# A hybrid decoder layer on one core: the hand order of its mixers, with pieces of projections between the instructions of each recurrent step and more of them behind substitutions and decode attention

## The chip, the core and the metric

The kernel runs on one core of a Trainium2 chip. The core has a matmul engine (TensorE, PE in the profile; its weight loads are shown as PEld), a vector engine (VectorE, DVE), an activation engine (ScalarE, ACT), GpSimd (POOL) and SyncE (SP), which issues the DMAs. Each engine works through its own queue in order; semaphores tie the queues to each other. The metric is the device time of one execution in microseconds (us), as the median of several runs.

## The reference

One decoder layer of width 1024, for a prompt of 1024 tokens and for 8 decode requests of 8 tokens each, which share the weights (1088 columns of tokens in all):

```python
x = x + 0.5 * rms_norm(swiglu_ffn(rms_norm(x, ffn1_norm_pre), ffn1_w_up, ffn1_w_down), ffn1_norm_post)
m, nk, nv, nc, ns = parallel_mixers(rms_norm(x, mix_norm_pre), w_in, ...)
x = x + rms_norm(m, mix_norm_post)
x = x + 0.5 * rms_norm(swiglu_ffn(rms_norm(x, ffn2_norm_pre), ffn2_w_up, ffn2_w_down), ffn2_norm_post)
```

`parallel_mixers` projects h with one matrix into the attention's q, k, v, a gated DeltaNet's q, k, v (qkv), its output gate z, two small columns, and the gates gA and gB. Branch A is sliding-window attention (8 heads, 2 key heads, window 128, sinks); the decode requests attend to a cache. Branch B, for each of 4 heads of 128 channels:

```python
xb = silu(short_conv(qkvb, width 4))
a = strict_lower(k_beta @ k.T * decay) + eye          # within a chunk of tokens
k_cum, v_u = solve(a, [k_beta * exp(gc), v * beta])
def step(s, xs):                                       # from chunk to chunk
    v_new = v_u_n - k_cum_n @ s
    o = q_dec_n @ s + qk_n @ v_new
    s = s * g_tot_n + k_dec_n.T @ v_new
ob = rms_norm(o, dn_out_norm) * silu(z)
m = (sigmoid(gA) * (oA @ w_branch_a) + sigmoid(gB) * (oB @ w_branch_b)) @ w_out
```

All is float32.

## The kernel before

Tokens lie along the free dimension, in three column chunks, `CH`: 0 to 384, 384 to 768, 768 to 1088 (the last 64 are the decode tokens). A projection onto 128 channels is a *unit*: its weights are loaded (two DMAs), split into a high part (a cast on ACT, L115) and a remainder (a subtraction on DVE, L116), and for each chunk `gemm` (L134) makes three matmuls for each of 8 blocks of the width: L142, L143 and L144 in the profile. So a unit is 3 × 8 × 3 = 72 matmuls, of 384 or 320 columns.

The first feed-forward layer comes first, then the projections of attention's q, k, v; then the mixers; then the branches, the output projection, and the second feed-forward layer. The change touches the mixers alone.

In the mixers, PE's order is written out by hand (`tc.manual_schedule(engines={PE})`, L1421); the other engines' order is left to a scheduler, which sees PE's. Between the instructions of the chains PE is given pieces of projections from a queue: a list of generators, each one unit. `gemm_p` (L839) yields after every block of three matmuls with a cost of 0.0013 us per column and 0.04: 0.54 for 384 columns, 0.456 for 320. `fill(us)` (L844) takes pieces off the head of the queue until that many us are used up, by these costs, or the queue is empty. `finish` (L852) issues what is left of units. The units are of three kinds: `conv_unit` (a head's q, k or v: projection into `pa`, then on ACT and DVE the norm factor, the short convolution L872, L874, and a SiLU, L901, L902), `z_unit` (the output gate's projection, L915, L916), and `gate_unit` (gA, gB: a tanh on ACT, L930; in the third chunk DVE applies the norm factor first, L672).

The chains, in their order:

- `attention_prompt` (L1007): 16 items in 18 rounds; in a round the scores (`att_s`, L950), softmax on ACT and DVE (`softmax`, L821 to L833), transposes (`att_t`, L979) and the products with v (`att_v`, L995), of three successive items, and then a fill.
- `attention_sample` (L1020): decode attention. Four items with scores (L1033, L1034), two additions on DVE (L1036, L1037), and a softmax; a fill; transposes of the probabilities (L1046, L1047); a fill; the products (L1055 and on).
- For each of two pairs of heads, 0 and 1, then 2 and 3: `Head.first` (L1108: transposes of k at L1129 with the squares' sums on ACT, L1131, and DVE, L1132; decay matrices; products; the matrix of the triangular system); `invert` (L1387: the 32 × 32 blocks of both heads inverted by 31 dependent steps on DVE, a trip through DRAM, and a fill); `Head.second` (L1225: the rest of the inverse from L1237 on, the product at L1283, eight recurrent steps, the decode tokens' step, and the norm of the output with L1363, L1374 and L1376 to L1380).

`first` and `second` are generators. `together` (L1383) takes one step of either head in turn, and each `yield` gives the us of a fill: the larger of the two heads' numbers is filled once, after both.

A recurrent step c of one head has, on PE: L1305 (the state into v_new), L1297 (the next step's u), L1314 (k with v_new), L1323 and L1324 (the output). DVE makes the scaled v_new (L1307) which L1314 needs, and the new state (L1317, L1321 in the first step) which the output of the next and L1323 of the same buffer wait for; ACT copies v_new (L1309, needed by L1324) and the output (L1325). The instructions of the two heads alternate: one head writes the PSUM buffers `ph`, the other `py`. `pa` (three buffers) holds the projections.

Of the kernel before, what the change touches and what calls it, by code (L numbers as in the profile page):

```python
# [35 lines left out]
def body(ctx: ExitStack, tc: tile.TileContext, d):  # L36
# [766 lines left out]
    for hlf in range(2):  # L803
        ps = py()
        for j in range(4):
            n = hlf * 4 + j
# [30 lines left out]
    queue = []  # L837
# [6 lines left out]
    def fill(us):  # L844
        while us > 0 and queue:
            t = next(queue[0], None)
            if t is None:
                queue.pop(0)
            else:
                us -= t  # L850

    def finish(units):  # L852
        for u in units:
            if u in queue:
                queue.remove(u)
                drain(u)
# [150 lines left out]
    def attention_prompt():  # L1007
        n = len(items)
        for it in range(n + 2):
            if it < n:  # L1010
                att_s(it)
            if it >= 2:
                att_v(it - 2)
            if 1 <= it <= n:
                att_t(it - 1)
            fill(4.8 if it else 7.0)
        for t in range(4):
            nc.sync.dma_start(oad[t, :, :NPR], YA[t][:, :NPR])

    def attention_sample():  # L1020
# [5 lines left out]
        for it in range(4):  # L1026
# [3 lines left out]
            for b4 in range(4):  # L1030
                b = bg2 * 4 + b4
# [8 lines left out]
            softmax(sb.unsqueeze(1), vec[:, V_SKS + g2 : V_SKS + g2 + 1], st())  # L1040
        fill(8.0)
        ptbs = [YA[0][:, it * 256 : it * 256 + 256] for it in range(4)]
# [8 lines left out]
        for it in range(4):  # L1051
# [6 lines left out]
            for b4 in range(4):  # L1058
                b = bg2 * 4 + b4
# [38 lines left out]
    class Head:  # L1098
# [9 lines left out]
        def first(self):  # L1108
# [15 lines left out]
            for c0 in (0, 4, 8):  # L1124
                n = 4 if c0 < 8 else 1
# [26 lines left out]
            nc.scalar.activation(eR, QK[:, cs8], AF.Exp)  # L1152
            yield 2.0

# [15 lines left out]
            for j, c0 in enumerate((0, 4)):  # L1170
                D = Ds[j]
                pq, pt = pb(), pb()
                for i in range(4):
                    w, cs, ix = chunk_of(c0 + i, h)
                    nc.tensor.matmul(pq[:, i * P : i * P + P], kT_[:, cs], q[:, cs], start=True, stop=True)
                for i in range(4):
                    nc.tensor.transpose(pt[:, i * P : i * P + P], D[:, i * P : i * P + P], ident)
                nc.vector.tensor_tensor(out=wide(QK, c0), in0=pq, in1=D, op=ALU.mult)
                nc.scalar.copy(D, pt)
                nc.gpsimd.tensor_tensor(out=wide(q, c0), in0=wide(q, c0), in1=Es[j], op=ALU.mult)  # L1180
                yield 0.0
            for j, c0 in enumerate((0, 4)):
# [31 lines left out]
            nc.gpsimd.memset(U[:NSM, NPR:], 0.0)  # L1214
            yield 0.0
            for c0 in (0, 4, 8):
                n = 4 if c0 < 8 else 1
# [4 lines left out]
                nc.scalar.copy(wide(v, c0) if c0 < 8 else v8, p[:w, : n * P])  # L1222
            yield 0.0

        def second(self):  # L1225
# [8 lines left out]
            for j in range(2):  # L1234
# [3 lines left out]
                nc.scalar.copy(Xs[j], p1)  # L1238
            yield 0.0
            for j in range(2):  # L1240
# [7 lines left out]
                nc.vector.tensor_tensor(out=wide(L, 4 * j), in0=wide(L, 4 * j), in1=p3, op=ALU.subtract)  # L1248
            yield 0.0
            p4s = [pb(), pb()]  # L1250
            for j in range(2):
# [6 lines left out]
                nc.scalar.copy(Xh, p4[:64, 0:256].rearrange("p (i c) -> p i c", c=64))  # L1258
            yield 0.0
            for j in range(2):  # L1260
# [17 lines left out]
            nc.scalar.mul(U[:w, cs], U[:w, cs], bhr[:w, 8:9])  # L1278
            yield 2.0
            for j in range(2):  # L1280
# [6 lines left out]
            nc.scalar.mul(mq[:, :NSM], p5[:, :w], -1.0)  # L1287
            yield 0.0

# [9 lines left out]
            uv(0)  # L1299
            yield 0.0  # L1300
            for c in range(8):
                w, cs, ix = chunk_of(c, h)
                p = ps[c]
                if c > 0:
                    nc.tensor.matmul(p[:, 0:128], M[:, cs], S, start=False, stop=True)  # L1305
                vns = ar[:, c % 2, :]
                nc.vector.tensor_scalar_mul(vns, p[:, 0:128], tk["kds"][:, ix : ix + 1])  # L1307
                vn = ar[:, 2 + c % 2, :]
                nc.scalar.copy(vn, p[:, 0:128])  # L1309
                yield 0.0  # L1310
                if c < 7:
                    uv(c + 1)
                yield 0.0
                nc.tensor.matmul(p[:, 128:256], k[:, cs], vns, start=True, stop=True)  # L1314
                S2 = ar[:, 4 + c % 2, :]
                if c > 0:
                    nc.vector.scalar_tensor_tensor(  # L1317
                        out=S2, in0=S, scalar=tk["gtot"][:, ix : ix + 1], in1=p[:, 128:256], op0=ALU.mult, op1=ALU.add
                    )
                else:  # L1320
                    nc.vector.tensor_copy(S2, p[:, 128:256])  # L1321
                if c > 0:
                    nc.tensor.matmul(p[:, 256:384], S, q[:, cs], start=True, stop=False)  # L1323
                nc.tensor.matmul(p[:, 256:384], vn, QK[:, cs], start=c == 0, stop=True)  # L1324
                nc.scalar.copy(QK[:, cs], p[:, 256:384])  # L1325
                S = S2
                yield 0.0
            nc.sync.dma_start(d["dpo"][h], S)
# [10 lines left out]
            nc.scalar.copy(ar[:, 0, :], p[:, 0:128])  # L1339
            yield 0.0  # L1340
            po = pb()
# [8 lines left out]
            for hf, vm in enumerate(vms):  # L1350
# [5 lines left out]
                )  # L1356
            yield 2.0
            nc.tensor.matmul(po[:, 128:192], vn, QK[:NSM, ss], start=True, stop=True)
# [11 lines left out]
            nc.sync.dma_start(d["dso"][:, h].rearrange("b p e -> p b e"), S0)  # L1370
            yield 5.0
            for a, b in ((0, 512), (512, 1024), (1024, NT)):
# [7 lines left out]
            nc.sync.dma_start(obd[h], QK)  # L1380
            yield 0.0

    def together(a, b):  # L1383
        for us in zip(a, b):
            fill(max(us))

    def invert(heads):  # L1387

        a, b = heads
# [17 lines left out]
        for i, x in enumerate(heads):  # L1407
# [6 lines left out]
            for b2 in range(2):  # L1414
                nc.sync.dma_start(U[32 * b2 : 32 * b2 + 32, NPR + 32 * b2 : NPR + 32 * b2 + 32], bu[h][32 + b2])
        fill(46.0)

# [3 lines left out]
    with tc.manual_schedule(engines={mybir.EngineType.PE}):  # L1421
        queue += zs[0:2] + gates[0:3] + heads[0].conv
        attention_prompt()
        attention_sample()
        queue += heads[1].conv
        for hs in (heads[0:2], heads[2:4]):
            finish(list(queue))
            queue += gates[3:9] if hs[0].h == 0 else gates[9:]
            together(*(x.first() for x in hs))
            invert(hs)  # L1430
            together(*(x.second() for x in hs))
            if hs[0].h == 0:
                finish(list(queue))
                queue += zs[2:4] + heads[2].conv + heads[3].conv
        finish(list(queue))
        wg4 = [unit(U_GA + i, f"ga{i}") for i in range(14, 16)]
        for c in range(3):
            for i in range(2):
                drain(gate_do(14 + i, wg4[i], c))
# [198 lines left out]
```

## Time and profile before

| | |
|---|---|
| median of 3 runs | 2466.16 us (2465.65 to 2466.87) |
| the profiled execution | 2460.59 us |
| its span, first to last instruction | 2458.8 us |
| mean granted clock of TensorE | 0.986 |
| prompt attention ends (last L995) | 973 us |
| decode attention, L1033 to the products | 1000 to 1020 us |
| first pair: first(), substitution, steps, tail | 1056.8 to 1206.2 us |
| between the pairs (gates, z, conv of heads 2 and 3) | 1206.2 to 1316.1 us |
| second pair | 1316.1 to 1463.2 us |

The profile's page gives each engine's busy time and the granted clock in 40 slices of 61 us; other views of the same trace group instructions by line, list what an engine waited for, give an engine's instructions in order of time, or sum each engine's busy time within stretches. Two peculiarities: matmuls are pipelined, so that the next one starts before the modelled end of the last, and durations of single matmuls overlap; starts are the safer measure. And a line of a helper (L142 to L144, L115, L116, L672) stands for all its callers; the tile's name (`h_ga`, `h_qkv`, `h_z`) tells them apart.

### The profile page before, as it was taken

How to read it: one execution, taken by the hardware profiler on the slowest of the kernel's cores; microseconds unless marked ns; L12 is line 12 of the kernel's file. 1: busy time of each engine (PE TensorE's matmuls, PEld its weight loads, DVE VectorE, ACT ScalarE, POOL GpSimd, SP SyncE). 2: the span in 40 equal slices, each digit the busy share in tenths (PEclk: the TensorE clock that was granted, in tenths of full speed). 3: DMA queues.
4: the chain of work that ended last, by engine and by line, in shares of the span. 5: the costliest groups of instructions: out<-in, count | busy, mean ns of one | idle time of the engine just before them, and what ended most of it. 6: DMA issues, size and time to landing. Idle time of an engine off the chain costs nothing. (4 is left out here: it accounts for less than half of the span.)

```text
span 2458.8 us, 38753 instructions
## 1 busy us (share of the span) xinstructions
PE 2372.7 (96%) x14535; PEld 2302.1 (94%) x14535; DVE 1691.8 (69%) x3385; ACT 1098.7 (45%) x2272; POOL 42.9 (2%) x33
## 2 busy tenths in 40 slices
PE   8999999999999999898999989999999999999997
PEld 7999999999998988898899879999989999999997
DVE  8887667767688467774477537655897476676677
ACT  7644424324466455443444343255654333233344
POOL 0000000000000000010101010000000000000000
PEclk9999999999999999899999999999999999999998
DMA  7332212213454411323322426435523122122453
GB/s 268 124 113 86 74 48 86 74 48 116 156 168 153 163 57 51 100 75 93 119 81 69 115 78 214 143 133 177 184 89 105 40 88 80 40 89 80 149 165 135
DMA packets 170373, 272.00 MB, mean 111 GB/s; under 512 B 34892, under 2 KB 74288, under 8 KB 170176
## 3 DMA queue, kind: packets, MB, share of 16 engines
q1 hardware_dynamic: 170184, 269.52, 34.1%
q8 instruction: 114, 1.87, 0.3%
q14 instruction: 75, 0.61, 0.1%
HBM read 227.03 MB, written 43.41 MB: 110 GB/s over the span
## 5 line engine op out<-in xcount | busy, mean ns | idle before, releaser
L467 PE MATMUL pa<-cl,h_c_s 128*128 128x384 f32 x704 | 236.3, 336 | 4.7 <-DVE cl L276 4.7
L466 PE MATMUL pa<-ch,h_c_s 128*128 128x384 f32 x704 | 237.3, 337 | 2.2 <-DVE t L472 1.8
L468 PE MATMUL pa<-ch,l_c_s 128*128 128x384 f32 x704 | 236.3, 336 | 0.0
L472 DVE TENSOR_TENSOR t<-pa,t 128x384 f32<-128x384 f32 x308 | 170.3, 554 | 85.1 <-PE pa L468 84.7
L466 PE MATMUL pa<-ch,h_c_a 128*128 128x384 f32 x528 | 177.2, 336 | 1.5 <-DVE t L472 0.8
L468 PE MATMUL pa<-ch,l_c_a 128*128 128x384 f32 x528 | 176.7, 335 | 0.0
L467 PE MATMUL pa<-cl,h_c_a 128*128 128x384 f32 x528 | 176.6, 334 | 0.0
L115 ACT CAST h_c_a<-r_c_a 128x512 fp32r<-128x512 f32 x132 | 81.8, 620 | 130.9 <-PE pa L467 107.7
L466 PEld LDWEIGHTS pa<-ch,h_c_s 128*128 128x128 f32 x704 | 132.9, 189 | 5.8 <-DVE t L472 5.5
L467 PEld LDWEIGHTS pa<-cl,h_c_s 128*128 128x128 f32 x704 | 133.0, 189 | 4.9 <-DVE cl L276 4.9
L468 PEld LDWEIGHTS pa<-ch,l_c_s 128*128 128x128 f32 x704 | 132.9, 189 | 0.0
L115 ACT CAST h_c_s<-q_c_s 128x512 fp32r<-128x512 f32 x132 | 82.0, 621 | 107.3 <-PE pa L467 96.8
L142 PE MATMUL pa<-xbh,h_ga 128*128 128x384 f32 (+1 forms) x384 | 128.3, 334 | 0.0
L144 PE MATMUL pa<-xbh,l_ga 128*128 128x384 f32 (+1 forms) x384 | 126.4, 329 | 0.0
L143 PE MATMUL pa<-xbl,h_ga 128*128 128x384 f32 (+1 forms) x384 | 126.3, 329 | 0.0
L466 PEld LDWEIGHTS pa<-ch,h_c_a 128*128 128x128 f32 x528 | 99.1, 188 | 2.8 <-DVE t L472 1.5
L467 PEld LDWEIGHTS pa<-cl,h_c_a 128*128 128x128 f32 x528 | 99.1, 188 | 0.0
L468 PEld LDWEIGHTS pa<-ch,l_c_a 128*128 128x128 f32 x528 | 99.1, 188 | 0.0
L142 PE MATMUL pa<-xbh,h_qkv 128*128 128x384 f32 (+1 forms) x288 | 95.9, 333 | 0.0
L143 PE MATMUL pa<-xbl,h_qkv 128*128 128x384 f32 (+1 forms) x288 | 95.0, 330 | 0.0
L144 PE MATMUL pa<-xbh,l_qkv 128*128 128x384 f32 (+1 forms) x288 | 94.9, 330 | 0.0
L115 ACT CAST h_c_s<-r_c_s 128x512 fp32r<-128x512 f32 x44 | 27.4, 622 | 147.9 <-PE pa L467 135.8
(630 smaller groups left out, 7271.0 us busy)
## 6 DMA issues: line engine op xcount, KB each, us to landing
r_c_a<-in_up_dram SPq DMA_DIRECT2D x132, 256.0 KB
q_c_a<-in_up_dram SPq DMA_DIRECT2D x44, 256.0 KB
q_ub<-in_up_dram SPq DMA_DIRECT2D x44, 256.0 KB
r_ub<-in_up_dram SPq DMA_DIRECT2D x44, 256.0 KB
r_ua<-in_up_dram SPq DMA_DIRECT2D x42, 256.0 KB
q_ua<-in_up_dram SPq DMA_DIRECT2D x42, 256.0 KB
r_da<-in_dn_dram SPq DMA_DIRECT2D x40, 256.0 KB
q_da<-in_dn_dram SPq DMA_DIRECT2D x40, 256.0 KB
```

The costliest lines, as they stand in the source:

```text
L115: nc.scalar.copy(hi, full)
L142: nc.tensor.matmul(ps[:, :n], hi[:, j, :], at(xh, k), start=first, stop=False)
L143: nc.tensor.matmul(ps[:, :n], hi[:, j, :], at(xl, k), start=False, stop=False)
L144: mm = nc.tensor.matmul(ps[:, :n], lo[:, j, :], at(xh, k), start=False, stop=last)
L466: nc.tensor.matmul(ps, wh[:, k, :], xh[:, k, :], start=k == 0, stop=False)
L467: nc.tensor.matmul(ps, wh[:, k, :], xl[:, k, :], start=False, stop=False)
L468: nc.tensor.matmul(ps, wl[:, k, :], xh[:, k, :], start=False, stop=k == 3)
L472: nc.vector.tensor_tensor(out=out, in0=ps, in1=other, op=ALU.add)
```

## The change

Five things are changed, all in the order of PE's instructions. No instruction is added or removed.

1. The fills of `attention_prompt` are 7.5 us in the first round and in the last two, 4.8 in the others.
2. One more gate unit is queued ahead of `attention_sample`, whose fill after the scores goes from 8 to 13 us; what is left in the queue then is issued before head 1's conv units are queued.
3. `together` fills after either head's step: a `yield` now carries two numbers, of which the first counts after head a and the second after head b. `first` has (2.0, 2.0) where it had one 2.0 for the pair; the steps of `second` get (0, 0.8) ahead of L1314 and (0, 0.5) at the end of a step, where nothing was filled; the fill before L1283 goes from 2.0 to 2.8.
4. The fill of `invert` goes from 46 to 51 us.
5. The queue of the first pair is gate units 4 to 9 (3 to 8 before), that of the second is the z units of heads 2 and 3 and gate units 10 to 13 (9 to 13 before); these z units no longer stand ahead of the conv units of heads 2 and 3.

```diff
-            fill(4.8 if it else 7.0)
+            fill(4.8 if 0 < it < n else 7.5)
...
-        fill(8.0)
+        fill(13.0)
...
             nc.scalar.activation(eR, QK[:, cs8], AF.Exp)
-            yield 2.0
+            yield 2.0, 2.0
...
             nc.scalar.mul(U[:w, cs], U[:w, cs], bhr[:w, 8:9])
-            yield 2.0
+            yield 0.0, 2.8
...
                 vn = ar[:, 2 + c % 2, :]
                 nc.scalar.copy(vn, p[:, 0:128])
-                yield 0.0
+                yield 0.0, 0.0
                 if c < 7:
                     uv(c + 1)
-                yield 0.0
+                yield 0.0, 0.8
                 nc.tensor.matmul(p[:, 128:256], k[:, cs], vns, start=True, stop=True)
...
                 S = S2
-                yield 0.0
+                yield 0.0, 0.5
             nc.sync.dma_start(d["dpo"][h], S)
...
-            yield 2.0
+            yield 0.0, 2.0
             nc.tensor.matmul(po[:, 128:192], vn, QK[:NSM, ss], start=True, stop=True)
...
-            yield 5.0
+            yield 0.0, 5.0
             for a, b in ((0, 512), (512, 1024), (1024, NT)):
...
     def together(a, b):
-        for us in zip(a, b):
-            fill(max(us))
+
+        for us in a:
+            fill(us[0])
+            fill(next(b)[1])
...
-        fill(46.0)
+        fill(51.0)
...
         attention_prompt()
+        queue += gates[3:4]
         attention_sample()
+        finish(list(queue))
         queue += heads[1].conv
         for hs in (heads[0:2], heads[2:4]):
             finish(list(queue))
-            queue += gates[3:9] if hs[0].h == 0 else gates[9:]
+            queue += gates[4:10] if hs[0].h == 0 else zs[2:4] + gates[10:14]
             together(*(x.first() for x in hs))
             invert(hs)
             together(*(x.second() for x in hs))
             if hs[0].h == 0:
                 finish(list(queue))
-                queue += zs[2:4] + heads[2].conv + heads[3].conv
+                queue += heads[2].conv + heads[3].conv
```

Every other `yield 0.0` of the two generators becomes `yield 0.0, 0.0`.

How the rows move is shown at three places. The first is a recurrent step of the first pair (c = 1) on PE. The names: `ph` is the PSUM buffer of head 0 and `py` that of head 1; `s_` are buffers in SBUF; `xbh`, `xbl` are the two parts of the normed input, `h_ga`, `l_ga` those of a gate unit's weights. Before:

```order
L1305 MATMUL ph_12195<-s_8355,s_8351 128x128
L1305 MATMUL py_12197<-s_8347,s_8345 128x128
L1297 MATMUL ph_12213<-s_8350,s_8353 128x128
L1297 MATMUL py_12215<-s_8344,s_8341 128x128
L1314 MATMUL ph_12195<-s_8355,s_8352 128x128
L1323 MATMUL ph_12195<-s_8348,s_8355 128x128
L1324 MATMUL ph_12195<-s_8354,s_8355 128x128
L1314 MATMUL py_12197<-s_8347,s_8340 128x128
L1323 MATMUL py_12197<-s_8342,s_8347 128x128
L1324 MATMUL py_12197<-s_8346,s_8347 128x128
```

The same step in the changed kernel, from L1297 to the second head's L1314:

```order
L1297 MATMUL ph_12375<-s_8350,s_8353 128x128
L1297 MATMUL py_12377<-s_8344,s_8341 128x128
L142 MATMUL pa_12298<-xbh_1_8284,h_ga_1_12096 128x320
L143 MATMUL pa_12298<-xbl_1_8286,h_ga_1_12096 128x320
L144 MATMUL pa_12298<-xbh_1_8284,l_ga_1_12097 128x320
L142 MATMUL pa_12298<-xbh_1_8284,h_ga_1_12096 128x320
L143 MATMUL pa_12298<-xbl_1_8286,h_ga_1_12096 128x320
L144 MATMUL pa_12298<-xbh_1_8284,l_ga_1_12097 128x320
L1314 MATMUL ph_12345<-s_8355,s_8352 128x128
L1323 MATMUL ph_12345<-s_8348,s_8355 128x128
L1324 MATMUL ph_12345<-s_8354,s_8355 128x128
L1314 MATMUL py_12347<-s_8347,s_8340 128x128
```

Six projection matmuls have come between L1297 and L1314 (three to six more follow the second head's L1324); between L1314 and L1323 there is none, before or now.

The second place is the tail of the first pair on PE, behind the decode tokens' products of L1366; `eye_72` holds the ones of L1374. Before, the 30 matmuls of a gate unit stood there, of which these are the last, and further ones behind L1374:

```order
L142 MATMUL pa_12453<-xbh_0_8283,h_ga_0_12135 128x320
L143 MATMUL pa_12453<-xbl_0_8285,h_ga_0_12135 128x320
L144 MATMUL pa_12453<-xbh_0_8283,l_ga_0_12136 128x320
L1374 MATMUL ph_12457<-s_8348,eye_72 128x512
L1374 MATMUL py_12460<-s_8348,eye_72 128x512
L1374 MATMUL ph_12463<-s_8348,eye_72 128x64
L1374 MATMUL py_12473<-s_8342,eye_72 128x512
L1374 MATMUL ph_12476<-s_8342,eye_72 128x512
L1374 MATMUL py_12479<-s_8342,eye_72 128x64
L142 MATMUL pa_12453<-xbh_0_8283,h_ga_0_12135 128x320
L143 MATMUL pa_12453<-xbl_0_8285,h_ga_0_12135 128x320
```

Now:

```order
L1366 MATMUL ph_12669<-s_8340,k_11427 128x512
L1366 MATMUL py_12672<-s_8340,k_11427 128x512
L1374 MATMUL ph_12676<-s_8348,eye_72 128x512
L1374 MATMUL py_12679<-s_8348,eye_72 128x512
L1374 MATMUL ph_12682<-s_8348,eye_72 128x64
L1374 MATMUL py_12692<-s_8342,eye_72 128x512
L1374 MATMUL ph_12695<-s_8342,eye_72 128x512
L1374 MATMUL py_12698<-s_8342,eye_72 128x64
L142 MATMUL pa_12720<-xbh_0_7321,h_qkv_0_12710 128x384
L143 MATMUL pa_12720<-xbl_0_7323,h_qkv_0_12710 128x384
L144 MATMUL pa_12720<-xbh_0_7321,l_qkv_0_12711 128x384
```

The queue is empty there, so L1374 follows L1366 at once, and the conv units of heads 2 and 3 (`h_qkv`, 432 matmuls) follow L1374, where 237 matmuls of gate and z units stood before.

The third place is DVE's queue at the first scores of decode attention; `st` are the softmax's small columns, `t_` and `s_8350` belong to a conv unit. Before:

```order
L1036 TENSOR_TENSOR s_8346<-ph_10675,cst 128x128
L902 SCALAR_TENSOR_TENSOR s_8350<-t_886_10621,t_885_10616 128x384
L874 SCALAR_TENSOR_TENSOR t_890_10660<-t_889_10656,vec,t_890_10660 128x384
L1037 TENSOR_TENSOR s_8346<-ph_10675,cst 128x64
L874 SCALAR_TENSOR_TENSOR t_890_10660<-t_889_10656,vec,t_890_10660 128x384
L824 TENSOR_REDUCE st_10686<-s_8346 128x1
L874 SCALAR_TENSOR_TENSOR t_890_10660<-t_889_10656,vec,t_890_10660 128x384
L825 TENSOR_TENSOR st_10686<-st_10686,vec 128x1
L116 TENSOR_TENSOR l_ga_0_11351<-r_ga_0_11348,h_ga_0_11350 128x512
L902 SCALAR_TENSOR_TENSOR s_8350<-t_891_10665,t_890_10660 128x384
L826 TENSOR_TENSOR st_10686<-vec,st_10686 128x1
```

Now:

```order
L1036 TENSOR_TENSOR s_8346<-ph_10751,cst 128x128
L896 TENSOR_SCALAR t_894_10695<-t_892_10686,vec 128x64
L1037 TENSOR_TENSOR s_8346<-ph_10751,cst 128x64
L897 TENSOR_TENSOR t_893_10690<-t_893_10690,t_894_10695 128x64
L824 TENSOR_REDUCE st_10762<-s_8346 128x1
L896 TENSOR_SCALAR t_894_10695<-t_892_10686,vec 128x64
L825 TENSOR_TENSOR st_10762<-st_10762,vec 128x1
L1036 TENSOR_TENSOR s_8346<-py_10772,cst 128x128
L897 TENSOR_TENSOR t_893_10690<-t_893_10690,t_894_10695 128x64
L826 TENSOR_TENSOR st_10762<-vec,st_10762 128x1
```

The wide conv rows (128x384) that alternated with the softmax now stand ahead of it or are done; narrow ones (128x64) are left between.

More of the change, by code (lines that the diff above doesn't have):

```diff
@@ L1214, in first @@
             nc.gpsimd.memset(U[:NSM, NPR:], 0.0)
-            yield 0.0
+            yield 0.0, 0.0
             for c0 in (0, 4, 8):
@@ L1222, in first @@
                 nc.scalar.copy(wide(v, c0) if c0 < 8 else v8, p[:w, : n * P])
-            yield 0.0
+            yield 0.0, 0.0
         def second(self):
@@ L1238, in second @@
                 nc.scalar.copy(Xs[j], p1)
-            yield 0.0
+            yield 0.0, 0.0
             for j in range(2):
@@ L1248, in second @@
                 nc.vector.tensor_tensor(out=wide(L, 4 * j), in0=wide(L, 4 * j), in1=p3, op=ALU.subtract)
-            yield 0.0
+            yield 0.0, 0.0
             p4s = [pb(), pb()]
@@ L1258, in second @@
                 nc.scalar.copy(Xh, p4[:64, 0:256].rearrange("p (i c) -> p i c", c=64))
-            yield 0.0
+            yield 0.0, 0.0
             for j in range(2):
@@ L1287, in second @@
             nc.scalar.mul(mq[:, :NSM], p5[:, :w], -1.0)
-            yield 0.0
+            yield 0.0, 0.0
             S0 = L[:, :NPR].rearrange("p (b e) -> p b e", e=P)
@@ L1299, in second @@
             uv(0)
-            yield 0.0
+            yield 0.0, 0.0
             for c in range(8):
@@ L1309, in second @@
                 nc.scalar.copy(vn, p[:, 0:128])
-                yield 0.0
+                yield 0.0, 0.0
                 if c < 7:
                     uv(c + 1)
-                yield 0.0
+                yield 0.0, 0.8
                 nc.tensor.matmul(p[:, 128:256], k[:, cs], vns, start=True, stop=True)
@@ L1326, in second @@
                 S = S2
-                yield 0.0
+                yield 0.0, 0.5
             nc.sync.dma_start(d["dpo"][h], S)
@@ L1339, in second @@
             nc.scalar.copy(ar[:, 0, :], p[:, 0:128])
-            yield 0.0
+            yield 0.0, 0.0
             po = pb()
@@ L1380, in second @@
             nc.sync.dma_start(obd[h], QK)
-            yield 0.0
+            yield 0.0, 0.0
     def together(a, b):
-        for us in zip(a, b):
-            fill(max(us))
+        for us in a:
+            fill(us[0])
+            fill(next(b)[1])
     def invert(heads):
```

## The prediction

> **What bounds the kernel now.** I read the page first: engine shares, then the forty slices.
>
> ```profile
> span 2458.8 us, 38753 instructions
> PE 2372.7 (96%) x14535; PEld 2302.1 (94%) x14535; DVE 1691.8 (69%) x3385; ACT 1098.7 (45%) x2272; POOL 42.9 (2%) x33
> PE   8999999999999999898999989999999999999997
> PEclk9999999999999999899999999999999999999998
> ```
>
> TensorE (PE) is busy 96% of the span, and VectorE (DVE) 69%. The change adds no matmul and takes none away: it only deals out the same projection pieces at other places. So it can gain only time in which PE stands still or runs at a low clock, and that time lies in slices 15 to 24 (61 us each), the mixers, where the digits fall below 9. For what PE waits there I read the list of its waits over 900 to 1480 us (what waits, for what, total us, times, longest us).
>
> ```profile
> PE ph L1237 <- DMA s<-ud: 7.3, 4, 2.9
> PE ph L1323 <- DVE s L1317: 6.2, 14, 0.4
> PE py L1323 <- DVE s L1317: 6.2, 14, 0.4
> PE ph L1046 <- DVE s L833: 3.9, 1, 3.9
> PE py L1046 <- DVE st L826: 2.3, 1, 2.3
> PE py L1129 <- ACT s L1131: 1.9, 2, 0.9
> PE ph L1129 <- ACT s L1131: 1.9, 2, 0.9
> PE ph L1314 <- ACT s L1309: 1.1, 2, 0.6
> PE ph L1283 <- ACT s L1284: 1.1, 2, 0.5
> ...
> PE py L1046 <- DVE s L833: 0.3, 1, 0.3
> PE ph L1046 <- DVE st L831: 0.3, 1, 0.3
> ```
>
> These are the dependent chains: the substitution's result (L1237), the recurrent steps (L1314, L1323), the softmax of decode attention (L1046), the head's norms (L1129). Third, the same stretches as windows: from:to and us; busy us with instruction count of PE, PEld, DVE, ACT and POOL; granted clock; DMA share and GB/s.
>
> ```profile
> 1008.84:1022.49 13.65, 10.84 (x55) 8.05 (x55) 7.98 (x45) 5.74 (x22) 0.00 (x0) 0.50 0.22 69
> 1056.80:1077.30 20.50, 17.45 (x140) 15.62 (x138) 19.87 (x67) 12.93 (x32) 6.12 (x5) 1.00 0.14 35
> 1077.30:1121.70 44.40, 44.40 (x270) 44.40 (x271) 26.56 (x73) 11.54 (x21) 3.78 (x2) 1.00 0.36 107
> 1128.30:1131.71 3.41, 3.41 (x18) 3.41 (x18) 0.25 (x1) 1.40 (x3) 0.00 (x0) 0.50 0.83 296
> 1149.85:1181.58 31.73, 23.43 (x153) 18.86 (x153) 10.32 (x32) 8.62 (x33) 0.00 (x0) 1.00 0.11 38
> 1182.91:1193.15 10.24, 10.23 (x40) 9.19 (x39) 3.09 (x6) 1.05 (x4) 3.79 (x2) 0.50 0.34 110
> 1199.91:1319.92 120.01, 118.44 (x714) 116.04 (x713) 85.54 (x230) 64.00 (x116) 6.69 (x6) 1.00 0.29 97
> 1244.94:1316.11 71.17, 71.17 (x435) 71.17 (x434) 58.98 (x177) 31.99 (x60) 1.63 (x4) 1.00 0.20 65
> 1445.74:1449.15 3.41, 3.40 (x12) 2.99 (x13) 2.17 (x5) 0.78 (x3) 1.90 (x1) 0.50 0.77 257
> ```
>
> Four of them stand at clock 0.50, each at or behind a long wait or a run of thin matmuls. The prices of a piece and of a gap come from PE's timeline (start, length in us, instruction, idle before it and its releaser).
>
> ```profile
> 1008.45 0.30 PE L1046 MATMUL ph<-eye,s 128*128 128x128 f32 x1 [3.87 <-DVE s L833]
> 1011.12 0.45 PE L1046 MATMUL py<-eye,s 128*128 128x128 f32 x1 [2.26 <-DVE st L826]
> ...
> 1157.80 0.39 PE L1297 MATMUL ph<-s,s 128*128 128x128 f32 x2
> 1158.02 0.39 PE L1297 MATMUL py<-s,s 128*128 128x128 f32 x2
> 1158.54 0.49 PE L1314 MATMUL ph<-s,s 128*128 128x128 f32 x2
> 1159.47 0.49 PE L1323 MATMUL ph<-s,s 128*128 128x128 f32 x2 [0.44 <-DVE s L1317]
> ...
> 1177.76 0.39 PE L1305 MATMUL py<-s,s 128*128 128x128 f32 x2
> 1178.72 0.49 PE L1314 MATMUL ph<-s,s 128*128 128x128 f32 x2 [0.57 <-ACT s L1309]
> ...
> 1320.27 0.42 PE L142 MATMUL pa<-xbh,h_ga 128*128 128x384 f32 x1
> 1320.53 0.34 PE L143 MATMUL pa<-xbl,h_ga 128*128 128x384 f32 x1
> 1320.70 0.33 PE L144 MATMUL pa<-xbh,l_ga 128*128 128x384 f32 x1
> ```
>
> From start to start a projection matmul takes 0.17 us at 384 columns (1320.53 to 1320.70), and 0.26 when it is the first of a group (1320.27 to 1320.53): **entering a group of pieces costs 0.1 us**. The 120.01 us window holds 714 instructions, mostly projections, and gives the same 0.17. At 320 columns I take 0.147 (44.40 us for 270 of both widths bears it out). Ends are modelled, so gaps are counted from starts: two passes of a step follow each other in 0.22 us (1157.80 to 1158.02).
>
> **The change part by part** (gains +). The profiled execution took 2460.59 us, 5.6 below the median 2466.16 of the timed runs; the terms are of that execution, and their sum is taken off the median.
>
> *A. Attention's end.* The fills of its first and its last two rounds become 7.5 us (7.0 and 4.8 before). The wait at L979 comes from DVE's softmax, and the longer fill brings evacuations into DVE's queue ahead of it. −0.9, an estimate of two such rows of 0.45 us (L672, below); bounds −2 and +2.
>
> *B. Decode attention.* Behind the scores stood 18 projection matmuls (2.6 us), then the queue was empty: the two waits of 3.87 and 2.26 us follow, and two of 0.3, 6.7 in all. Now 54 stand there, 30 at 384 and 24 at 320 columns: 8.7 us, 6.1 more. DVE's queue is lightened as well: the conv rows that stood among its softmax rows are thinned out. So I let all of the 6.7 go. The low clock behind it goes with it: in the 13.65 us the same transposes last 0.45 us where 0.30 stood at full clock; for the 55 instructions there I take 1.9, since most of them are thin and wait anyway. **+8.6**; bounds +5.9 (waits shorten by 6.1 less two entries, clock stays) and +10.
>
> *C. The split fill in first().* Twelve matmuls (2.1 us) now stand between the two heads' transposes, at which PE waited 3.8 us over both pairs. For the first pair **+1.9**; bounds 0 and 3 (17.45 busy in 20.50).
>
> *D. Substitution, first pair.* 300 matmuls instead of 270 lie behind it: 204 × 0.173 + 96 × 0.147 = 49.4 us, 5.0 more.
>
> ```profile
> 1122.61 1.13 PE L1237 MATMUL ph<-s,s 128*128 128x128 f32 x8 [0.59 <-DMA s<-ud]
> ...
> 1384.13 1.89 PE L1237 MATMUL ph<-s,s 128*128 128x128 f32 x8 [2.46 <-DMA s<-ud]
> ```
>
> The four waits of L1237 sum to 7.3: 0.59 and 2.86 in the first pair, 2.46 and 1.40 in the second. Five more us of pieces cover either pair. Behind the 2.86 stand 3.41 us at clock 0.50, 18 instructions; at full clock half of that, less what waits anyway: 1.3. 0.6 + 2.9 + 1.3 = **+4.8**; bounds +3 and +5.2.
>
> *E. Before L1283* a few more pieces: the wait of 1.1 over both pairs goes. **+1.1**; bounds 0 and 1.5.
>
> *F. The steps.* Six matmuls (1.04 us) now stand ahead of L1314, three to six behind L1324. The gap before L1314 is 0.52 − 0.22 = 0.3 us, and a restart after a gap costs 0.1 (0.49 against 0.39 of length). It goes in 14 steps; two entries of 0.1 come: 14 × (0.4 − 0.2) = 2.8. In the eighth step of each pair the gap is 0.96 − 0.22 = 0.74: 2 × 0.64 = 1.3. The larger gaps, L1314 to L1323 (12.4 us in the list of waits), get **nothing**: no piece stands between these lines. Against it stand three DVE rows of the pieces per pair (L116 twice, L672) which now lie between L1307 and L1317; half of them at the wrong moment cost 1.4. **+2.7**; bounds −6 and +5.
>
> *G. The tail.* The queue is empty after L1342, so the fill of 5.0 us behind L1366 gets nothing. L1374 must wait for the sum of squares of head b (L1363) where projections stood. Head a's is done when PE gets there; its L1374 takes 1.9 us, and b's is done about 0.8 us later. **−1.5** for two pairs; bounds −4 and 0.
>
> *H. The second pair, first() and substitution.* The z units and a gate unit leave the stretch between the tail and first(): PE has 432 conv matmuls, 71.0 us, and 3 of L1374, 74 in all. DVE keeps nearly all of its work.
>
> ```profile
> L116 DVE TENSOR_TENSOR l_ga<-r_ga,h_ga 128x512 fp32r<-128x512 f32 x7 | 4.8, 688 | 0.0
> L672 DVE SCALAR_TENSOR_TENSOR t<-pa,r 128x256 f32<-128x256 f32 (+1 forms) x9 | 4.1, 452 | 0.6 <-PE pa L144 0.6
> L916 DVE SCALAR_TENSOR_TENSOR t<-t,t 128x384 f32<-128x384 f32 (+1 forms) x6 | 3.2, 534 | 6.3 <-ACT t L915 6.3
> ```
>
> Of 85.5 us in the 120 us from L1363 to first()'s first reduction leave eight L116, four L672 and six L916: 5.5 + 1.8 + 3.2, so 75.0 us are left against 74 on PE. DVE becomes the bound here. It was at 58.98 of 71.17 = 0.83 in the conv stretch, and at 19.87 of 20.50 = 0.97 in first(); I take 0.90, between these, as it is now never starved. 75.0 / 0.90 = 83.3: first()'s reductions start 9.3 us behind PE's arrival, where it was 3.8 (1316.11 to 1319.92). Of the 5.5 more, the split fill takes 2.1: −3.4. The substitution's 3.9 goes as in D with a low clock of 1.9 (8 passes took 1.89 us instead of 1.13). **+2.4**; bounds −6 and +6.
>
> *J. Conv of heads 2 and 3 right behind the tail.* Its casts on ScalarE and DVE compete with the norms of the tail; the first two casts stand ahead of these in the order. An estimate of two L116 rows: −1.5; bounds −5 and 0. *K. What follows the mixers* starts after a shorter tail (144 matmuls instead of 165); taken as 0, bounds −3 and +3.
>
> Sum: −0.9 + 8.6 + 1.9 + 4.8 + 1.1 + 2.7 − 1.5 + 2.4 − 1.5 = 17.6, so 2466.2 − 17.6 = **2448.6**.
>
> **The rivals.**
>
> *R1, the clock.* After either pair's steps stand thin matmuls (L1336) at clock 0.50: 10.24 us in the first pair, 3.41 in the second. The steps before them were 23.43 of 31.73 = 0.74 busy; with 12.7 us of pieces in them they become about 36 of 42 = 0.87. If that keeps the clock full, half of 13.65 comes on top, 6.8: **2441.8**. Against it: L1336 itself stays as thin as it was. [...]
>
> *R2, slower: the DVE backlog of H.* If DVE keeps the density of the whole old stretch, 85.54 of 120.01 = 0.71, it needs 75.0 / 0.71 = 105.6 us: 31.6 behind PE, 22.3 more than forecast, and with a low clock after so long a wait (half of a 6.8 us stretch) **2474**. It decides below a density of 75 / (74 + 9.3 + 17.6) = 0.74. For it: PE gives it less cover. Against it: the old density was low because PE was the bound. At 0.83 it gives 90.4, 7.1 more: **2456** (R2').
>
> *R3, the steps pay nothing.* The pieces only displace: no gain at the gap, two entries each, and all three DVE and five ScalarE rows per pair (about 4.5 us) delay the chain L1307 → L1314 → L1317 → L1323. F becomes −3 − 9 × 0.6 = about −8: **2459**. The steps' waits at L1323 would then have grown. For it: the order puts them there, and each engine works in order. Against it: L1309's copy has over 1 us of slack until L1324.
>
> *R4, no effect:* DVE limits the mixers as a whole, and each gap closed reopens at the next wait: **2466**. Against it, DVE is at 69%.
>
> **How the numbers follow.** Forecast 0.47 (2444 to 2454), R1 0.17, R2' 0.13, R3 0.12, R4 0.06, R2 0.05. The last two, and the edge of the others, are left out of the range: 2437 to 2461, which also takes in the bounds of B, F and H taken together by half. A measurement of this kernel can tell about 0.2%, 4.9 us, from no change. Faster, under 2461.2: 0.47 + 0.17 + 0.13 + two thirds of R3 = 0.85; same 0.10; slower 0.05.
>
> **What would show it.** B: L1046 without idle before it, and no 0.50 around it. D and H: L1237 without idle. F: L1314 without a gap, L1323 still with 0.44. G: an idle of under 1 us before head b's L1374. H: DVE almost full from L1374 to first(), and longer waits of L1129 in the second pair than in the first. R1 shows in the clock at L1336. Wrong would be: waits at `pa` in the conv stretch (DVE or ScalarE holding the buffers back), or longer waits at L1323.

## The result and the profile after

The changed kernel takes 2444.9 us (median of 4 runs, 2439.4 to 2447.5), before 2466.2: **a ratio of 0.9911, interval 0.9893 to 0.9928**, 21.3 us faster. The forecast was 17.6 us. Its profiled execution is one of the four, the slowest (2447.49), 13.1 below that of before; why the medians lie further apart is said with the clock, below.

The page of the changed kernel, the lines that stood in the prediction:

```profile
span 2445.6 us, 38753 instructions
PE 2368.5 (97%) x14535; PEld 2300.2 (94%) x14535; DVE 1690.9 (69%) x3385; ACT 1091.3 (45%) x2268; POOL 44.2 (2%) x33
PE   8999999999999999999899999999989999999997
PEclk9999999999999999999999989999999999999998
```

No instruction of the kernel was added or removed (the trace has 37 loads of ACT's tables where it had 41, which is why ACT counts four fewer). PE stands still for 77 us of its span instead of 86. Its waits in the mixers (900 to 1480 us):

```profile
PE ph L1323 <- DVE s L1317: 6.5, 14, 0.6
PE py L1323 <- DVE s L1317: 6.2, 14, 0.4
PE ph L1186 <- DVE s L1178: 4.2, 2, 2.2
PE ph L979 <- DVE s L833: 3.5, 1, 3.5
PE ph L1129 <- ACT s L1131: 2.3, 1, 2.3
PE py L1129 <- ACT s L1131: 1.6, 2, 0.9
...
PE py L1374 <- DVE s L1363: 0.5, 1, 0.5
```

L1237, L1046, L1283 and L1314 are gone from the list. L1323 is as it was, L1186 is new, and L1129 has lost nothing (3.8 us before, 3.9 now). The windows of the same trace, columns as in the prediction: the steps of the first pair, the conv stretch of heads 2 and 3, the second first(), a half-clock stretch over the second pair's tail, and the stretch from the end of L1363 to first()'s first reduction on DVE, which is the last row.

```profile
1158.15:1194.38 36.23, 29.88 (x204) 27.21 (x203) 10.13 (x30) 9.45 (x32) 0.00 (x0) 1.00 0.20 60
1212.80:1284.69 71.89, 71.11 (x432) 70.82 (x431) 66.48 (x189) 38.97 (x74) 7.87 (x5) 1.00 0.23 78
1284.69:1314.40 29.71, 23.88 (x151) 21.79 (x149) 24.59 (x75) 15.67 (x38) 7.10 (x6) 0.83 0.21 65
1431.09:1448.16 17.07, 17.06 (x39) 9.60 (x38) 9.59 (x16) 4.78 (x8) 2.15 (x2) 0.50 0.51 164
1210.44:1292.17 81.73, 77.83 (x467) 76.01 (x467) 73.29 (x213) 47.30 (x90) 8.01 (x6) 0.99 0.26 88
```

DVE is now 0.92 busy in the conv stretch (0.83 before) and late at first(): its first reduction starts 7.5 us behind PE's arrival (1284.69 to 1292.17), where it was 3.8.

```profile
1292.17 0.68 DVE L1132 TENSOR_REDUCE nk<-s 128x4 f32<-128x512 f32 x1
```

This first() lasts 29.7 us, 10.2 of them at half clock; the first pair's lasts 23.0, all at full clock.

To see where the time went I take, for each matmul, the time from its start to the next one's start less the usual distance for that shape (lower quartile in the trace of before), and sum this **excess** over a stretch. Moved pieces don't disturb it.

| stretch on PE | excess before | after | gain | forecast |
|---|---|---|---|---|
| prompt attention to L1033 (A) | 16.9 | 16.0 | +0.9 | −0.9 |
| decode attention (B) | 8.0 | −2.4 | +10.4 | +8.6 |
| first(), first pair (C) | 3.7 | 4.2 | −0.5 | +1.9 |
| substitution to steps, first pair (D, E) | 8.9 | 2.3 | +6.6 | +5.3 |
| the same, second pair (H, E) | 9.3 | 2.3 | +7.0 | +6.4 |
| steps, both pairs (F) | 26.0 | 20.3 | +5.7 | +2.7 |
| L1336 to L1358, both pairs | 7.0 | 4.8 | +2.2 | 0 |
| tail, both pairs (G) | 1.3 | 8.8 | −7.5 | −1.5 |
| conv of heads 2 and 3 (J) | 0.5 | 1.4 | −0.9 | −1.5 |
| first(), second pair (H) | 4.1 | 10.9 | −6.9 | −3.4 |
| 60 us behind the mixers (K) | 4.6 | 7.2 | −2.6 | 0 |

The column of gains, with −1.2 of the rest, gives the 13.2 us by which the span is shorter.

### The profile page after: what moved, and what is told of

Same layout as the page of the kernel before. It is cut to its first block, busy times and chain, and to the rows that moved or that the text cites. A ratio compares the mean times of both kernels' runs of the same rounds, so it can differ in the third digit from the quotient of the medians.

```text
span 2445.6 us, 38753 instructions
## 1 busy us (share of the span) xinstructions
PE 2368.5 (97%) x14535; PEld 2300.2 (94%) x14535; DVE 1690.9 (69%) x3385; ACT 1091.3 (45%) x2268; POOL 44.2 (2%) x33
```

## The experiments

**Theory.** The gains are the covered waits of L1046 and L1237 and the gap ahead of L1314; they are partly paid back where the queue runs dry (tail) and where PE no longer covers DVE (the second first()). **Rivals.** The pieces in the steps only displace; or the losses have other causes. Lines are those of the changed kernel before an edit.

**The same kernel again**, for its spread.

> The changed kernel again, nothing edited. Its four runs so far spread from 2439.4 to 2447.5 us, where those of before spread by 1.2, and the mean granted clock went from 0.986 in the slowest to 0.990 in the fastest. Theory (the free half-clock stretches now fall on dense or on thin work from run to run): the median stays at 2445 within 3 us, and the time falls by about 2 us for each 0.001 of clock. Rival (something else differs from run to run, such as a transfer): the spread is as wide, but time and clock do not go together.

Measured: 2444.9 (2434.7 to 2452.8, 6 runs); ratio 0.9906, 0.9878 to 0.9935. 2434.71 us went with a mean clock of 0.992, 2452.81 with 0.982: 1.8 us per 0.001, correlation −0.99. The kernel before did the same over 51 runs (2458.6 to 2477.7, 2.3 us per 0.001, −0.91). So the spread goes with the time at half clock (the clock is 1.00 or 0.50 in the traces of both kernels, with 71 of 2445.6 us at 0.50 in that of the change). It also explains the medians: the profiled execution of before had clock 0.986, the median of its runs 0.984, so it lay well below its median; that of the changed kernel was its longest of four. A line through each kernel's runs, read at clock 0.986, compares without that chance:

| kernel | median us | median clock | at clock 0.986 |
|---|---|---|---|
| before (51 runs) | 2466.7 | 0.984 | 2462.0 |
| the change (10 runs) | 2444.9 | 0.987 | 2446.2 |
| decode attention alone | 2458.2 | 0.984 | 2456.3 |
| substitution alone | 2463.2 | 0.984 | 2458.2 |
| the change, bare steps | 2440.0 | 0.989 | 2448.3 |
| bare steps, dry tail | 2448.2 | 0.986 | 2447.0 |
| z units back | 2453.2 | 0.986 | 2453.2 |

At equal clock 16 us of the change's gain are left; the other 5 to 6 go with a higher clock.

**One part alone.** Decode attention's fills on the kernel before:

> The kernel before with the fills of the prompt's ends and of decode attention alone (7.5, 13, gate unit 3 ahead of it, the rest issued behind it). Theory (the waits of L1046 and the half clock behind them go, and do not come back): 2466.2 - 10 = 2456, no idle at L1046, no half-clock stretch of 13.65 us. Rival (DVE's rows of the softmax and conv units only end later, and first() of the first pair waits for them instead): 2462 to 2466, with more waiting at L1129 and L1186.

```diff
-            fill(4.8 if it else 7.0)
+            fill(4.8 if 0 < it < n else 7.5)
...
-        fill(8.0)
+        fill(13.0)
...
         attention_prompt()
+        queue += gates[3:4]
         attention_sample()
+        finish(list(queue))
         queue += heads[1].conv
...
-            queue += gates[3:9] if hs[0].h == 0 else gates[9:]
+            queue += gates[4:9] if hs[0].h == 0 else gates[9:]
```

Measured: 2458.2, ratio 0.9962 (0.9943 to 0.998). L1046 has no wait, the excess of decode attention falls by 10.5 us, and what stood at L1129 before (3.8 us) still stands there, no more: the rival falls. The total of the profiled run shows nothing of it (2461.7 us, 1.1 more than that of before), because its tails ran 27.3 and 17.1 us at half clock (10.2 and 3.4 in the profile of before). The first of them:

```profile
1178.41:1205.72 27.31, 26.86 (x83) 20.90 (x84) 8.95 (x15) 4.30 (x9) 3.79 (x2) 0.50 0.28 84
```

These tails were not dry: 30 projection matmuls stand ahead of L1374 in either, as in the kernel before.

The substitution's fill at 51 on the kernel before:

> The kernel before with the substitution's fill at 51 instead of 46 alone. Theory (the four waits of L1237, 7.3 us, and the half clock behind them, 2 to 3 us, go): 2466.2 - 10 = 2456, L1237 without waits. Rival (the pieces' own rows on DVE delay the 31 steps by as much): waits of 3 us or more are left at L1237, 2461 to 2466.

Measured: 2463.2, ratio 0.998 (0.9965 to 0.9995). One wait of L1237 is left:

```profile
PE ph L1237 <- DMA s<-ud: 0.9, 1, 0.9
```

From the substitution to the steps its profiled run gains 6.1 and 5.4 us in the two pairs. The theory's place is right, its total is not: it lies in the rival's range. The tails of that run, with 33 and 24 projections ahead of L1374, stood at half clock for 20.5 us each and took it back; over its ten runs 3.5 us are gained against the median of before, 4.9 by the ratio, and why it is not more stays open. By their ratios the two parts alone give 14 of the change's 21 to 23 us; the rest was not run by itself.

**The steps.** Both fills to 0:

> The changed kernel without pieces in the recurrent steps (both fills 0); the pieces go to the fills behind L1342 and L1366 and behind L1374. Theory (the gap ahead of L1314 and the wait in the eighth step are what pays, 2.8 us a pair in the trace; the tail gets back its cover, 1 to 2 us a pair): 2444.9 + 5.7 - 3 = 2447.6, the windows of the steps return to an excess of 13.0 us from 10.2. Rival (the pieces in the steps pay nothing, they only displace): 2442 to 2444.

```diff
-                yield 0.0, 0.8
+                yield 0.0, 0.0
...
-                yield 0.0, 0.5
+                yield 0.0, 0.0
```

Measured: 2440.0 (2434.0 to 2445.9), ratio to before 0.9892 (0.9871 to 0.9914), 5 us *below* the change, though the intervals overlap. In the bare kernel, the steps, the second first() and the second tail:

```profile
1156.04:1184.22 28.18, 20.75 (x138) 16.74 (x137) 9.12 (x28) 7.40 (x28) 0.00 (x0) 1.00 0.13 42
1284.30:1309.30 25.00, 21.17 (x152) 18.95 (x151) 22.37 (x70) 13.81 (x34) 7.64 (x5) 0.93 0.19 55
1412.81:1434.42 21.61, 21.60 (x109) 16.71 (x107) 10.25 (x17) 8.00 (x15) 3.79 (x2) 0.92 0.48 145
```

The steps take 28.2 us, and 36.2 with 10.9 us of pieces in them (48 matmuls at 0.173 and 18 at 0.147): the pieces gain 3 us a pair, as the theory has it. But the second first() is 4.7 us shorter without them, and the tails' excess goes from 2.5 and 6.3 to 0.7 each. So neither total is met: the steps' gain is there, as the theory says, and the rest of the program loses as much and more, which is past even the rival. The 5 us by which the bare kernel is ahead are not clear of the spread of either kernel's runs. Two causes are possible, told apart by leaving the tail empty in the bare kernel (L1357 and L1371 to 0 as well):

> Bare steps, and also nothing in the fills behind L1342 and L1366 (0 instead of 2.0 and 5.0): the 90 matmuls left stand behind L1374. It tells apart why the bare steps ran 5 us faster than the changed kernel. Theory a (an empty queue in the tail: its chain stands open and the clock stays halved there): about 2445, half-clock stretches of 10 us or more over L1336 to L1374, the tails' excess up from 0 to 2 to 6 us each. Theory b (only the cover behind L1374 counts, which lets DVE catch up before the second first()): about 2438, the tails' stretches short.

Measured: 2448.2 (2441.0 to 2450.6), ratio 0.9925 (0.9905 to 0.9945). Here its second first(), its second tail, and the half-clock stretch in it:

```profile
1289.90:1313.00 23.10, 19.61 (x150) 17.60 (x148) 21.94 (x69) 13.84 (x34) 6.65 (x5) 1.00 0.22 59
1416.54:1436.35 19.81, 19.07 (x64) 10.76 (x62) 8.52 (x14) 6.00 (x11) 3.79 (x2) 0.66 0.38 113
1420.21:1433.86 13.65, 12.91 (x23) 5.95 (x23) 8.52 (x14) 3.50 (x6) 2.05 (x2) 0.50 0.42 133
```

Theory a holds: with 90 matmuls behind L1374 first() gets shorter still (23.1 against 25.0), yet the kernel is 8 us slower, both tails stand 13.65 us at half clock, their excess is 6.7 and 6.5 us, and the median clock falls from 0.989 to 0.986. So of the two it is the empty tail that costs, and by its clock: read at clock 0.986 the two bare kernels are alike (2448.3 and 2447.0; the first is read beyond its runs, which lay at 0.987 to 0.991). But a full tail does not keep the clock up by itself: those of the decode-attention and substitution runs above held their projections and stood at half clock for 17 to 27 us.

**The second first().** The z units back ahead of the conv units, at the expense of the second pair's queue:

> The changed kernel with the z units of heads 2 and 3 again ahead of the conv units of heads 2 and 3; the second pair's queue is gate units 10 to 13 alone, so it runs dry in the second pair's substitution (264 matmuls instead of 300) and gives nothing to its steps. Theory (DVE falls behind PE in the conv stretch, which the moved z units leave shorter for PE): the excess of the second pair's first() falls from 10.9 us to 5 or less, L1129's wait of 2.3 goes; the dry queue costs 1 to 4 us at L1237, 1 at L1283 and 2.8 in the steps: about 2445 to 2449 in all. Rival (the wait in the second first() has another cause, such as the split fill or the casts): the excess there stays at 9 or more, 2452.

```diff
-            queue += gates[4:10] if hs[0].h == 0 else zs[2:4] + gates[10:14]
+            queue += gates[4:10] if hs[0].h == 0 else gates[10:14]
-                queue += heads[2].conv + heads[3].conv
+                queue += zs[2:4] + heads[2].conv + heads[3].conv
```

Measured: 2453.2, ratio 0.9947 (0.9928 to 0.9965). first() lasts 23.10 us again, its excess falls from 10.9 to 4.3: DVE's backlog came from the shorter stretch, as the theory says. In total it is 4 us worse than the theory's range, and past the rival's 2452: the dry queue cost 5.2 at L1237, 3.9 up to the steps, 2.8 in them.

**The wait that the change leaves**, L1323. One more yield, so that the heads alternate there too:

```diff
                 else:
                     nc.vector.tensor_copy(S2, p[:, 128:256])
+                yield 0.0, 0.0
                 if c > 0:
                     nc.tensor.matmul(p[:, 256:384], S, q[:, cs], start=True, stop=False)
```

On the change, on the bare steps, and on the kernel before:

> The changed kernel with one more yield, of no us, between L1314 and L1323, so that the heads alternate there too: L1314 of both heads, then L1323 and L1324 of either. Theory (the 28 waits of L1323 for L1317, 12.7 us, are a head's own chain; the other head's L1314 covers one of the two): 0.9 us in each of 14 steps, 12 us, or about 2433. Rival (the step is bound elsewhere, by the copies on ACT or by DVE's order): the steps shorten by less than 5 us, 2440 or more.

> The same yield, with no pieces in the steps at all. Theory (what the steps' pieces gain is lost again in the tail and in first(), so bare steps are the better base; the alternation gains the same 12 us on it): 2440.0 - 12 = 2428. Rival (with the heads alternating, the gap ahead of L1314 and L1323's remaining wait can only be filled by pieces): 2433 or more, no better than with pieces.

> The kernel before with the alternation of the heads between L1314 and L1323 alone. It tells whether the 12.7 us of waits at L1323, which the change leaves as they were, are worth the same without the rest of the change, and whether the rest of the alternation's gain of 20 us on the bare steps comes from the clock. Theory (0.9 us in 14 steps, and denser steps with shorter half-clock stretches behind them, at 2 us per 0.001 of mean clock): 2467 - 12 - 4 to 8 = 2447 to 2451, mean clock up by 0.002 or more. Rival (the clock gain belongs to the fuller tails of the bare kernel): 2455, clock unchanged.

Measured: **2431.7** (ratio 0.9858, 0.9836 to 0.9879), **2419.4** (0.9806, 0.9785 to 0.9827) and **2447.3** (0.9922, 0.9901 to 0.9942). A step of the bare alternating kernel, in which L1324 is what was L1323:

```profile
1159.36 0.39 PE L1297 MATMUL py<-s,s 128*128 128x128 f32 x2
1159.87 0.49 PE L1314 MATMUL ph<-s,s 128*128 128x128 f32 x2
1160.19 0.42 PE L1314 MATMUL py<-s,s 128*128 128x128 f32 x2
1160.80 0.49 PE L1324 MATMUL ph<-s,s 128*128 128x128 f32 x2 [0.18 <-DVE s L1317]
1161.12 0.39 PE L1325 MATMUL ph<-s,s 128*128 128x128 f32 x2
1161.35 0.39 PE L1324 MATMUL py<-s,s 128*128 128x128 f32 x2
```

The second head's L1314 stands in the first head's wait, and its own wait is gone. The steps of a pair go from 28.2 to 21.7 us: 13 us in all, on the bare kernel as on the kernel before. The rest of the 20.6 us on the bare kernel is the clock for 4 or 5 (0.989 to 0.991), and 3 I can't place. The theory holds on all three, the bare kernel even below its figure; on the kernel before the mean clock rose from 0.9837 to 0.9855. It beats both kernels of the case by 47 and 26 us, and the one line is worth, on the kernel before, nearly what the whole change is.

**Two more covers** on it: 15 matmuls ahead of L1186, then also the prompt's fill of 8.5 us one round earlier.

> The bare alternating kernel with 15 more projection matmuls (2.6 us) ahead of L1186, taken from the 45 left behind the tail. It tests why the split fill in first() gained nothing in the first pair: the wait at L1129 went, and 2.2 us stood at L1186, for DVE (L1178). Theory (DVE sets when L1186 can start; only more PE work ahead of it fills the time): both waits of L1186, 4.2 us, go, first()'s excess falls by 2 us a pair, 2419.4 - 3.5 = 2416. Rival (the evacuations of the added pieces and the shorter cover behind the tail push DVE back by as much): the wait shows up at L1129 of the second pair or at L1221, 2419 or more.

```diff
                 nc.gpsimd.tensor_tensor(out=wide(q, c0), in0=wide(q, c0), in1=Es[j], op=ALU.mult)
-                yield 0.0, 0.0
+                yield 0.0, 2.2 * j
```

> The same, and the prompt's fill of 8.5 us in the round that stands ahead of the last transposes (the last but two, 4.8 before) with 4.8 in the last two, where the change put 7.5. Theory (the change's longer fills stand behind the wait of L979, 3.5 us, and cannot cover it; this one stands ahead): L979's wait goes, 2416 - 3 = 2413. Rival (the wait is DVE's softmax, which the pieces' own evacuations delay): 3 us or more of wait stay at L979, 2416.

```diff
-            fill(4.8 if 0 < it < n else 7.5)
+            fill(8.5 if it in (0, n - 1) else 4.8)
```

Measured: 2424.7 (ratio 0.9834, 0.981 to 0.9859) and 2419.6 (0.9808, 0.9786 to 0.9831). L1186's waits go, but others come, in the first of the two:

```profile
PE py L1129 <- ACT s L1131: 1.7, 2, 0.9
PE ph L1129 <- ACT s L1131: 1.4, 1, 1.4
PE ph L1237 <- DMA s<-ud: 1.2, 1, 1.2
PE ph L1283 <- ACT s L1284: 1.0, 2, 0.5
```

Without the 15 matmuls L1129 had 1.5 us and the other two had none. In the first pair the cover does pay at its place: first() lasts 23.2 us with the 15 matmuls in it, 23.0 in the bare kernel without them. In the total the rival holds: nothing gained. At L979 3.3 us were left of 3.5, so the rival holds there too; that the second is 5 us below the first is as much as its clock (0.991 against 0.990) and chance explain.

## Why the prediction came out right, step by step

The direction, the time (2444.9 in 2437 to 2461, 3.7 us from the forecast) and the main terms were right. That the total came so close is in part luck. Between the two profiles some terms came 11 us better than forecast (F, L1336 to L1358, A, B, D and E most), others 16 us worse (G, H's first(), K and C most), which leaves 13.2 us where 17.6 were said. The medians lie 21.3 apart because the profile of before lay below its median and that of the changed kernel was the longest of four, which is chance too.

- **B, D, E, and L1237 in H: right, and larger than said** (24.0 against 20.3). The waits went and did not come back; both parts do it alone, at their places; in total the substitution's part alone brought half of what was expected or less. What was undersized was the half clock behind a wait: the waits themselves were 15.2 us, so some 9 came on top where 5.1 were taken (13.65, 3.41 and 3.41 us stood at 0.50 there before).
- **F: right in mechanism, mis-sized: +5.7 against +2.7.** Of the 1.4 us set aside for the pieces' DVE rows nothing was needed, nor all of the entries' cost. L1323 stayed as it was, as said. R3 (the pieces pay nothing in the steps) is refuted at its place: steps with pieces are 3 us shorter per pair than the pieces and the bare steps apart. Yet the pieces are missing elsewhere, and a kernel without them is no slower.
- **G: the wait was right, the size was not: −7.5 against −1.5.** The prediction priced the dry tail by its wait, L1363 (0.7 us of idle in all, better than said), and put nothing for the clock. By starts the first tail, at full clock throughout, lost 1.8 us and the second 5.7, and a run of 17 us at half clock lies on the second. In the other profile of the same kernel, from the run for its spread, that place has stretches of 3.4 and 6.8 us instead, so a part of the −7.5 is chance of the one execution.
- **H, first(): −6.9 against −3.4.** DVE is the bound there, as said, and no later than said: it was busy 0.90 of the stretch from L1363 to the first reduction (73.29 of 81.73 us; 0.90 was taken) and 7.5 us behind PE (9.3 was taken). What failed is the 2.1 us that the split fill was to save: as in C, a wait of 2.0 us at L1186 came in its place. And 10.2 us of this first() ran at half clock, for which there was no term. Bringing the z units back gave 6.6 us of it again. R2 (density 0.71) did not come.
- **C: wrong, −0.5 against +1.9.** In the first pair L1129 waits 1.2 us less and L1186, which waits for DVE (L1178), 2.2 more: the cover moved the wait. Cover ahead of L1186 took that wait away too, but gained nothing in the total.
- **A: wrong in sign, within 2 us**, and the added fill lies behind the wait of L979, which stayed (2.9 before, 3.5 now).
- **K: −2.6 where 0 was taken**, inside its bounds: 3.4 us at half clock and waits of 2.1 us for L672 have come there. That the shorter stretch ahead of the branches' first products brings them is not tested.
- **R1, the clock:** it was at 0.50 for 10.2 us behind the first pair's steps before and for 3.4 in the changed profile, but behind the second pair's for 3.4 before and 17 now. On average over the runs the clock rose by 0.003, 5 to 6 us, about what R1 named. That denser steps keep the clock full was the author's estimate, and no run shows it: the kernel with bare steps has a higher clock still (0.989). Which stretches the rise comes from is not shown, since only one or two executions of a kernel tell the clock by place.

## What to carry to other kernels

Before filling a wait with other work, see whether the other half of the same work can stand there: alternating two independent chains one instruction earlier was worth 13 us of PE time and more, at no cost in pieces, where pieces from a limited queue gained 6 in the same steps and were then missing in the tail. Count such pieces as a stock: each place filled is another one emptied, and the place that runs dry pays with its wait, with its cover for other engines, and here most of all with its clock (13.65 us at 0.50 in either tail of the bare kernel that had no pieces there). And where runs of one kernel spread by 10 us, compare over the runs and against their clock before reading a single profile's total.

## What the runs showed of the hardware

The half clock lasted through stretches in which PE was busy without a gap: 17.06 of 17.07 us in the changed kernel's second tail. Of the 13.4 us of it that lie ahead of L1374, 8.0 went to L1358 and L1366, which have half the rows (the first number of the weights' shape, 64 in `64*128`), and 3.5 to 12 projection matmuls of 128 rows; the rest was thin. In the dry-tail kernel:

```profile
1423.73 2.04 PE L1366 MATMUL ph<-s,k 64*128 64x512 f32 x2 [0.43 <-DVE s L1351]
1425.57 1.91 PE L1366 MATMUL py<-s,k 64*128 64x512 f32 x2
...
1427.60 2.02 PE L1366 MATMUL ph<-s,k 64*128 64x512 f32 x2
1429.41 1.91 PE L1366 MATMUL py<-s,k 64*128 64x512 f32 x2
1431.25 2.07 PE L1374 MATMUL ph<-s,eye 128*128 128x512 f32 x2
```

7.5 us of L1366 and L1358 (64 rows), back to back, left the clock at 0.50; it rose at 1433.86, 2.6 us after L1374 (128 rows) had begun. In the changed kernel it rose 3.7 us after, and not in the 3.5 us of projections. The stretches here are five and four times the 3.41 us of the shortest ones in the trace of before (17.07, 13.65). Whether the rows decide is not shown; that they do is the author's guess from these places, not tested by itself.
